# The second layer's FFN outputs: twelve of 22 k tiles by seven half-size products per pair of outputs

## The chip, the cores and the metric

The kernel runs on one core of a Trainium2 chip. The metric is the device time of one execution in microseconds (us); less is better. The engines named in the profile are TensorE (PE for its matrix products, PEld for its weight loads), VectorE (DVE), ScalarE (ACT), GpSimd (POOL) and SyncE (SP), whose queue issues most of the transfers.

## The reference, cut to what matters

A sequence of 512 tokens with 1024 features passes two layers. Each has a mixer (a gated recurrence in the first, chunked attention in the second) and a SwiGLU FFN with 2816 hidden features, each behind a norm with shift, scale and gate from a conditioning vector. A final norm gives the output. The part that matters here is the FFN of the second layer and what follows it:

```python
def swiglu(u, w_in, w_out):
    gate, up = jnp.split(u @ w_in, 2, axis=-1)
    return (jax.nn.silu(gate) * up) @ w_out
...
h = h + g2[:, None, :] * swiglu(u, ffn_w_in[layer], ffn_w_out[layer])
...
return rms_norm(h, final_norm)
```

## The kernel before

Activations lie transposed: 128 features by 512 tokens to a tile. The residual stream is eight such tiles, `h[0]` to `h[7]`; the hidden layer has 22 (`FT`), which are the k tiles of the output product. An fp32 product is made of three matmuls (`mm3`, lines 188 to 193): the weight and the activation are each split into a rounded high part and a low rest, and high·high, high·low and low·high are added into one PSUM bank. The high part is a copy on ScalarE, the low part a subtraction on VectorE (`split`, lines 124 to 137; for activations `parts`, lines 467 to 478).

Weights follow one list, `weight_plan`. `load` issues their transfers on SP's queue two ahead into a ring of three `raw` buffers; `fetch` splits them one ahead into rings of three `wh` and three `wl` buffers; `weight` hands out the next one split, and `take` hands one out raw. For one hidden tile per layer (`by_transfer`, line 120) the low part is made otherwise: ScalarE writes the negated raw weight to `wl`, and a transfer on POOL's queue adds the raw weight to it in memory (lines 131 and 132).

The FFN inputs of hidden tiles 4 to 21 (`fast_tiles`, lines 516 to 606) already use a scheme of seven products: the contraction and the tokens are cut in two, sums of weight blocks and of activation blocks are formed, and seven products with 256 tokens replace eight. Products 1 to 7 add into three banks in an order in which a bank is read by ScalarE or VectorE after each product and then added onto. Their weight buffers start at an offset of 16 elements (`NEAR`), and every fourth tile uses 24 (`APART`) for one product (line 547).

The FFN outputs (lines 480 to 513) are plain: outputs 0 and 1 run together over the 22 k tiles while those are split, then outputs 2 to 7 one after another, each from three weight chunks of 8, 8 and 6 k tiles. `residual` (line 356) adds the gated bank onto `h[n]`. `finish` (line 1382) squares the new `h[n]` into the sum for the final norm and scales the late tokens by the norm's gain (`gained`). The last output is done in two halves of the tokens: while the second half (256 products of tokens `CUT` to 511) runs, the norm of the first half is taken at its k tile 3 (`mean`) and multiplied and written at k tile 11 (`write`). `last_tokens` then transposes and writes the late tokens.

The order of instructions on each engine is made by a scheduler at build time, from priorities and dependencies; `tc.issue_after(x)` puts instructions behind x on their engine. `mods_after` in `state` is a marker of that kind.

## Time and profile before

| what | value |
|---|---|
| median of 3 runs | 1227.47 us (1226.13 to 1227.63) |
| the profiled execution | 1225.95 us, its span 1224.0 us |
| TensorE busy | 1209.0 us, 99% of the span |
| VectorE busy | 984.8 us, 80% |
| ScalarE busy | 648.4 us, 53% |
| POOL busy | 20.6 us, 2% |
| mean transfer rate | 145 GB/s, 177.55 MB |
| last fast input product, by the timeline | 1092.5 us |
| first product of the closing norm | 1214.86 us |

Matmuls overlap each other in the records, so the time of one product is read from the distance of two starts, not from its duration. A group of instructions is shown with its line, engine and operation, its operands with shapes, its count, its busy time in us and the mean of one in ns, and then the idle time ahead of it and what ended that. In the timeline a row is a start, a length, the instruction, and in brackets the idle time before it.

### The profile page before, as it was taken

How to read it: one execution, taken by the hardware profiler on the slowest of the kernel's cores; microseconds unless marked ns; L12 is line 12 of the kernel's file. 1: busy time of each engine (PE TensorE's matmuls, PEld its weight loads, DVE VectorE, ACT ScalarE, POOL GpSimd, SP SyncE). 2: the span in 40 equal slices, each digit the busy share in tenths (PEclk: the TensorE clock that was granted, in tenths of full speed). 3: DMA queues.
4: the chain of work that ended last, by engine and by line, in shares of the span. 5: the costliest groups of instructions: out<-in, count | busy, mean ns of one | idle time of the engine just before them, and what ended most of it. 6: DMA issues, size and time to landing. Idle time of an engine off the chain costs nothing.

```text
span 1224.0 us, 21555 instructions
## 1 busy us (share of the span) xinstructions
PE 1209.0 (99%) x8548; PEld 1049.3 (86%) x8548; DVE 984.8 (80%) x1769; ACT 648.4 (53%) x1157; POOL 20.6 (2%) x29
## 2 busy tenths in 40 slices
PE   8999999999999999999999999999999999999997
PEld 7887788788899999988888877777889999998887
DVE  8996778977989999987669878996798999984333
ACT  6455446443656666742228566665465666673221
POOL 0000000000000000000000000000000000000000
PEclk9999999999999999999999999999999999999999
DMA  9642354463424444568751445431243433343321
GB/s 352 255 132 97 112 183 156 155 208 121 119 91 154 155 139 141 173 208 277 235 170 69 138 139 167 164 100 58 93 120 106 153 139 138 106 128 97 100 88 69
DMA packets 52532, 177.55 MB, mean 145 GB/s; under 512 B 5968, under 2 KB 8400, under 8 KB 52432
## 3 DMA queue, kind: packets, MB, share of 16 engines
q1 hardware_dynamic: 51856, 174.08, 41.9%
q0 software_dynamic: 576, 2.10, 1.0%
q8 instruction: 67, 1.10, 0.4%
q14 instruction: 33, 0.27, 0.1%
HBM read 171.96 MB, written 2.10 MB: 142 GB/s over the span
## 4 chain that ended last, share of the span: by engine, by line
PE 90%; DVE 5%; ACT 3%; issue 1%; DMA 1%; SPq 0%; POOL 0%; DVEq 0%; POOLq 0%; ACTq 0%
PE f_r L561 9%; PE f_r L560 9%; PE f_r L559 9%; PE f_o L193 6%; PE f_o L192 6%; PE f_o L191 6%; PE f L191 2%; PE f L193 2%; PE f L192 2%; PE o L859 1%; PE bo L1271 1%; PE bo L191 1%; PE av L214 1%; PE bo L193 1%; PE bo L192 1%; PE ao L191 1%
## 5 line engine op out<-in xcount | busy, mean ns | idle before, releaser
L561 PE MATMUL f_r<-f_h,f_w_l 128*128 128x256 f32 x1008 | 279.0, 277 | 0.0
L559 PE MATMUL f_r<-f_h,f_w_h 128*128 128x256 f32 x1008 | 278.7, 277 | 0.0
L560 PE MATMUL f_r<-f_l,f_w_h 128*128 128x256 f32 x1008 | 278.7, 277 | 0.0
L561 PEld LDWEIGHTS f_r<-f_h,f_w_l 128*128 128x128 f32 x1008 | 189.3, 188 | 0.4 <-DVE f_w_l L525 0.4
L560 PEld LDWEIGHTS f_r<-f_l,f_w_h 128*128 128x128 f32 x1008 | 189.5, 188 | 0.1
L559 PEld LDWEIGHTS f_r<-f_h,f_w_h 128*128 128x128 f32 x1008 | 189.3, 188 | 0.1
L192 PE MATMUL f_o<-f_p,f_o_h 128*128 128x512 f32 (+1 forms) x374 | 141.1, 377 | 0.1
L193 PE MATMUL f_o<-f_p,f_o_l 128*128 128x512 f32 (+1 forms) x374 | 141.2, 378 | 0.0
L191 PE MATMUL f_o<-f_p,f_o_h 128*128 128x512 f32 (+1 forms) x374 | 140.8, 377 | 0.0
L127 ACT ACTIVATE f_o_h<-r_f_o 128x1024 fp32r<-128x1024 f32 (+1 forms) x48 | 46.8, 987 | 131.5 <-PE f_o L192 98.2
L341 DVE SCALAR_TENSOR_TENSOR mw<-mw,crow 128x1024 f32<-128x1024 f32 x96 | 115.3, 1217 | 0.7 <-DMA mw<-in_modw 0.7
L134 DVE TENSOR_TENSOR f_o_l<-r_f_o,f_o_h 128x1024 fp32r<-128x1024 f32 (+1 forms) x48 | 54.1, 1132 | 67.9 <-ACT f_o_h L127 60.4
L524 ACT ACTIVATE f_w_h<-f_x 128x1024 fp32r<-128x1024 f32 x72 | 76.7, 1065 | 46.1 <-PE f_r L560 39.0
L525 DVE TENSOR_TENSOR f_w_l<-f_x,f_w_h 128x1024 fp32r<-128x1024 f32 x72 | 87.8, 1224 | 4.8 <-ACT f_w_h L524 2.4
L524 ACT ACTIVATE f_w_h<-r_f_c 128x1024 fp32r<-128x1024 f32 x72 | 61.1, 849 | 46.0 <-PE f_r L560 44.9
L193 PEld LDWEIGHTS f_o<-f_p,f_o_l 128*128 128x128 f32 x374 | 70.3, 188 | 14.3 <-DVE f_o_l L134 1.5
L192 PEld LDWEIGHTS f_o<-f_p,f_o_h 128*128 128x128 f32 x374 | 70.4, 188 | 13.3 <-DVE f_p L476 0.6
L191 PEld LDWEIGHTS f_o<-f_p,f_o_h 128*128 128x128 f32 x374 | 70.4, 188 | 12.8
L525 DVE TENSOR_TENSOR f_w_l<-r_f_c,f_w_h 128x1024 fp32r<-128x1024 f32 x72 | 68.5, 951 | 5.8 <-ACT f_w_h L524 5.8
L1246 ACT ACTIVATE sb<-sb,st 128x128 f32<-128x128 f32 (+1 forms) x64 | 35.8, 560 | 29.8 <-DVE st L1245 29.4
L762 DVE TENSOR_TENSOR kq<-kq,t 128x1024 f32<-128x1024 f32 x28 | 34.2, 1220 | 5.2 <-PE fine L786 2.6
L193 PE MATMUL f<-f_h,f_l 128*128 128x512 f32 x96 | 36.9, 391 | 0.0
(401 smaller groups left out, 2705.5 us busy)
## 6 DMA issues: line engine op xcount, KB each, us to landing
mw<-in_modw SPq DMA_DIRECT2D x96, 512.0 KB, 4.2
r_f_c<-in_ffn_in SPq DMA_DIRECT2D x72, 512.0 KB, 3.4
r_f_o<-in_ffn_out SPq DMA_DIRECT2D x32, 512.0 KB, 3.6
mrow<-in_modw SPq DMA_DIRECT2D x16, 512.0 KB, 8.5
r_f<-in_ffn_in SPq DMA_DIRECT2D x16, 512.0 KB, 3.4
r_f_o<-in_ffn_out SPq DMA_DIRECT2D x16, 384.0 KB, 3.4
r_av<-in_a_v SPq DMA_DIRECT2D x8, 512.0 KB, 4.6
r_g<-in_a_g SPq DMA_DIRECT2D x8, 512.0 KB, 3.3
```

What stands on the lines that cost most here:

```text
L127: A.activation(wh, raw, AF.Copy)
L134: low = V.tensor_sub(wl, raw, wh)
L191: T.matmul(ps, wh[:, kt, :], uh, start=start, stop=False)
L192: T.matmul(ps, wh[:, kt, :], ul, start=False, stop=False)
L193: T.matmul(ps, wl[:, kt, :], uh, start=False, stop=stop)
L341: V.scalar_tensor_tensor(mw, mw, 1.0, crow, op0=ALU.mult, op1=ALU.mult, accum_out=raw[:, j:j + 1])
L524: A.activation(wh, raw, AF.Copy)
L525: V.tensor_sub(wl, raw, wh)
L559: T.matmul(ps, wh[:, j, :], uh, start=f, stop=False, skip_group_check=True)
L560: T.matmul(ps, wh[:, j, :], ul, start=False, stop=False, skip_group_check=True)
L561: T.matmul(ps, wl[:, j, :], uh, start=False, stop=stop and j == 3, skip_group_check=True)
L1246: A.activation(s[:, 0:n], s[:, 0:n], AF.Exp, bias=st[:, 1:2], accum_out=st[:, 2:3])
```

## The change

Only the second layer's FFN outputs change (`OUT` = 1).

- K tiles 0 to 11 (`PAIRS` = 6 pairs) are done by seven half-size products for each pair of outputs (2i, 2i+1): the two outputs, the two k tiles of a pair and the two halves of the tokens are the blocks. Products 1, 5, 6, 2, 7, 3, 4 add into three banks r1, r2, r3; after each one VectorE adds the bank onto the one quarter of `h` that it belongs to, with the sign from `g2` or `ng2`.
- K tiles 12 to 21 stay plain, in two chunks of five. Outputs 0 and 1 run them together, then outputs 2 to 5 (their low weight parts now by adding transfers); then come the four pairs; then the plain part of outputs 6 and 7 (`HELD`) in halves of the tokens, early tokens of 7 and 6, then late tokens of 6 and 7.
- While outputs 2 to 5 run, `prepare_pairs` forms two sums (y0, y2) of activation quarters for each of the six pairs of k tiles, two quarters in each, and splits all seven operands.
- `weights` prepares seven weight operands per pair of outputs, three products ahead. Of their four sums, two are made by transfers (`load_sum`: SP loads one block from HBM into a tile, then a POOL transfer adds another block from HBM to it), two by VectorE. The next pair's sum is asked for once this pair's is used.
- The norm's `mean` comes at step 5 of the 20 steps of the last two half outputs (it was 3 of 22), `write` at step 11 as before. `gained` uses one tile for two outputs.
- The weights of k tiles 0 to 11 lie in HBM with the even k tiles first.

The diff, cut to its core:

```diff
-CUT, WRITE_AT = 256, 11
+CUT, MEAN_AT, WRITE_AT = 256, 5, 11
...
+OUT, PAIRS, CHUNK = 1, 6, 5
+HELD, FREE = (6, 7), 14
...
     def by_transfer(key):
+        if key[0] == f"f{OUT}" and key[1] == "o":
+            return 2 <= key[2] < HELD[0]
         return key[0] in [f"f{layer}" for layer in FAST] and key[1] == PLAIN - 1
     def split(raw, nk, n, nm, tag, key):
-        wh = wp.tile([P, nk, n], F32R, tag=tag + "h", name=f"{nm}_h")
-        wl = wp.tile([P, nk, n], F32R, tag=tag + "l", name=f"{nm}_l")
+        if key in spare:
+            wh, wl = spare.pop(key)()
+        elif key[:2] == (f"f{OUT}", "o") and key[2] in HELD:
+            wh, wl = (wp.tile([P, SHIFT + D], F32R, tag=tag + x, name=f"{nm}_{x}")[:, NEAR:NEAR + nk * n]
+                      .rearrange("p (k c) -> p k c", k=nk) for x in "hl")
+        else:
+            wh = wp.tile([P, nk, n], F32R, tag=tag + "h", name=f"{nm}_h")
+            wl = wp.tile([P, nk, n], F32R, tag=tag + "l", name=f"{nm}_l")
         A.activation(wh, raw, AF.Copy)
         state.pop("meanwhile", lambda: None)()
         if by_transfer(key):
             A.activation(wl, raw, AF.Copy, scale=-1.0)
-            G.dma_start(out=wl, in_=raw, accum_op=ALU.add)
+            state["moved"] = G.dma_start(out=wl, in_=raw, accum_op=ALU.add)
         else:
             low = V.tensor_sub(wl, raw, wh)
...
+            if layer == OUT:
+                drain(side)
+                fast_out(fp, nm, a, raw_a, FIRST, g2, finish)
+                return
...
+    def fast_out(fp, nm, a, raw_a, first, g2, finish):
+        H = S // 2
+        row1, row2 = slice(H, S), slice(0, H)
+        K0 = 2 * PAIRS
+        halves = (slice(0, CUT), slice(CUT, S))
+        room = [(cst, f"ul{i}", 1) for i in range(8)] + [(cst, "uh4", 1), (cst, "uh5", 1)]
+        room = [(fp, f"sp{i}", 1) for i in range(10)] + room + [(fp, "sp10", 1), (cst, "uh6", 1), (cst, "uh7", 1)]
+        room += [(mp, "mraw", 2), (mp, "mraw", 2), (mp, "crow", 2), (fp, "xs1", 4), (fp, "xs0", 4), (fp, "ab0", 2)]
+        units = []
+        def unit():
+            if not units:
+                pool, tag, m = room.pop(0)
+                kw = {"bufs": 2} if tag == "mraw" else {"bufs": 1}
+                t = pool.tile([P, m, S], F32R, tag=tag, name=f"{nm}_u{len(room)}", **kw)
+                units.extend(t[:, i, :] for i in range(m))
+            return units.pop(0)
+        def split_plain(k):
+            if not isinstance(a[k], tuple):
+                ah, al = unit(), unit()
+                A.activation(ah, a[k], AF.Copy)
+                with tc.issue_after(ends[min(FREE + k - K0, len(ends) - 1)].ins):
+                    V.tensor_sub(al, a[k], ah)
+                a[k] = ah, al
+            return a[k]
+        order = (2, 5, 3, 4, 0, 1)
+        sums_at = dict(zip(order, ("uo0", "uo1", "uo2", "uo3", "xs2", "xs3")))
+        slots = {}
+        def pair(j):
+            k = 2 * j
+            base = k if k < first else first + 4 * ((k - first) // 4)
+            return raw_a[base][:, k - base:k - base + 2, :]
+        def two(x):
+            return x.rearrange("p (a c) -> p a c", a=2)
+        def prepare_pairs():
+            for j in order:
+                r = pair(j)
+                y0 = sm.tile([P, 2, H], F32, tag="et", name=f"{nm}_y{j}", bufs=2)
+                y2 = sm.tile([P, 2, H], F32, tag="ut", name=f"{nm}_z{j}", bufs=2)
+                with tc.issue_after(state["mods_after"].ins):
+                    V.tensor_sub(y0[:, 0, :], r[:, 1, row2], r[:, 0, row2])
+                    V.scalar_tensor_tensor(y0[:, 1, :], y0[:, 0, :], -1.0, r[:, 0, row1], op0=ALU.mult, op1=ALU.subtract)
+                yield
+                with tc.issue_after(state["mods_after"].ins):
+                    V.tensor_sub(y2[:, 0, :], r[:, 0, row1], r[:, 0, row2])
+                    V.scalar_tensor_tensor(y2[:, 1, :], r[:, 1, row1], -1.0, y0[:, 1, :], op0=ALU.mult, op1=ALU.subtract)
+                yield
+                t = fp.tile([P, 8, H], F32R, tag=sums_at[j], name=f"{nm}_q{j}")
+                for i, y in enumerate((y0, y2)):
+                    A.activation(t[:, 2 * i:2 * i + 2, :], y, AF.Copy)
+                    V.tensor_sub(t[:, 4 + 2 * i:6 + 2 * i, :], y, t[:, 2 * i:2 * i + 2, :])
+                    yield
+                oh, ol, m = two(unit()), two(unit()), two(unit())
+                A.activation(oh, r[:, :, row1], AF.Copy)
+                A.activation(m[:, 0, :], r[:, 1, row2], AF.Copy)
+                with tc.issue_after(state["mods_after"].ins):
+                    V.tensor_sub(ol, r[:, :, row1], oh)
+                    V.tensor_sub(m[:, 1, :], r[:, 1, row2], m[:, 0, :])
+                slots[j] = {1: (oh[:, 0, :], ol[:, 0, :]), 3: (oh[:, 1, :], ol[:, 1, :]), 2: (m[:, 0, :], m[:, 1, :])}
+                slots[j].update({4 + i: (t[:, i, :], t[:, 4 + i, :]) for i in range(4)})
+                yield
+        ops = {}
+        def one(i, q, raw):
+            at = APART if q == 7 and i % 2 == 0 else NEAR
+            wh, wl = (wp.tile([P, SHIFT + D], F32R, tag="w" + x, name=f"{nm}_o{i}_{q}{x}")[:, at:at + PAIRS * P]
+                      .rearrange("p (j c) -> p j c", j=PAIRS) for x in "hl")
+            A.activation(wh, raw, AF.Copy)
+            V.tensor_sub(wl, raw, wh)
+            ops[i, q] = wh, wl
+        added = {}
+        def load_sum(i, q):
+            if i < 4:
+                t = fp.tile([P, PAIRS, P], F32, tag={1: "x2", 3: "ab2"}[q], name=f"{nm}_t{q}_{i}")
+                odd, even = slice(PAIRS, 2 * PAIRS), slice(0, PAIRS)
+                w = d["ffn_out"][OUT]
+                with tc.issue_after(state["asked"].ins):
+                    nc.sync.dma_start(t, w[2 * i + 1, :, even, :])
+                with tc.issue_after(state["moved"].ins):
+                    G.dma_start(out=t, in_=w[2 * i, :, even, :] if q == 1 else w[2 * i + 1, :, odd, :], accum_op=ALU.add)
+                added[i, q] = t
+        def weights(i):
+            def got(x):
+                return take((nm, "o", i, x))
+            one(i, 1, got("c11"))
+            yield
+            t1 = added.pop((i, 1))
+            one(i, 5, t1)
+            yield
+            b22 = got("c22")
+            t2 = fp.tile([P, PAIRS, P], F32, tag="x1", name=f"{nm}_t2_{i}")
+            V.tensor_add(t2, b22, t1)
+            one(i, 6, t2)
+            load_sum(i + 1, 1)
+            yield
+            b21 = got("c21")
+            one(i, 2, b21)
+            V.tensor_add(t2, b21, t2)
+            yield
+            one(i, 7, added.pop((i, 3)))
+            load_sum(i + 1, 3)
+            yield
+            one(i, 3, b22)
+            yield
+            one(i, 4, t2)
+            yield
+        def stream():
+            for i in range(4):
+                yield from weights(i)
+        chunks = stream()
+        done = {"n": 0}
+        def ahead(upto):
+            while done["n"] < upto and next(chunks, chunks) is not chunks:
+                done["n"] += 1
+        def product(i, q, ps, s, start):
+            wh, wl = ops.pop((i, q))
+            for j in range(PAIRS):
+                uh, ul = slots[j][s]
+                f = start and j == 0
+                T.matmul(ps, wh[:, j, :], uh, start=f, stop=False, skip_group_check=True)
+                T.matmul(ps, wh[:, j, :], ul, start=False, stop=False, skip_group_check=True)
+                T.matmul(ps, wl[:, j, :], uh, start=False, stop=j == PAIRS - 1, skip_group_check=True)
+        def onto(n, c, ps):
+            g = ng2 if n % 2 else g2
+            V.scalar_tensor_tensor(h[n][:, c], ps, g[:, n:n + 1], h[n][:, c], op0=ALU.mult, op1=ALU.add)
+        ng2 = cst.tile([P, KT], F32, tag="ng2", name="ng2")
+        with tc.issue_after(ends[-1].ins):
+            V.tensor_scalar_mul(ng2, g2, -1.0)
+        prep = prepare_pairs()
+        load_sum(0, 1)
+        pss = [bank(f"{nm}_o{n}_0") for n in range(2)]
+        for ci in range(2):
+            ws = [weight((nm, "o", n, ci)) for n in range(2)]
+            for kt in range(CHUNK):
+                k = K0 + CHUNK * ci + kt
+                for k2 in (k, min(k + 1, FT - 1)):
+                    split_plain(k2)
+                for w, ps in zip(ws, pss):
+                    mm3(ps, w, kt, a[k], k == K0, k == FT - 1)
+        for n, ps in enumerate(pss):
+            residual(n, ps, g2)
+        for n in range(2, HELD[0]):
+            ps = bank(f"{nm}_o{n}_0")
+            for ci in range(2):
+                w = weight((nm, "o", n, ci))
+                for kt in range(CHUNK):
+                    k = K0 + CHUNK * ci + kt
+                    mm3(ps, w, kt, a[k], k == K0, k == FT - 1)
+                    if kt != 2:
+                        next(prep, None)
+                    if n == HELD[0] - 1 and ci and kt in (1, 3):
+                        ahead((kt + 1) // 2)
+            residual(n, ps, g2)
+            if n == HELD[0] - 1:
+                load_sum(0, 3)
+        drain(prep)
+        def beside():
+            t = fp.tile([P, 2, D], F32R, tag="uo0", name=f"{nm}_o6_w")
+            return [t[:, e, NEAR:NEAR + CHUNK * P].rearrange("p (k c) -> p k c", k=CHUNK) for e in range(2)]
+        spare[nm, "o", HELD[0], 1] = beside
+        for i in range(4):
+            n0, n1 = 2 * i, 2 * i + 1
+            r1, r2, r3 = (bank(f"{nm}_or{q}_{i}")[:, 0:H] for q in (1, 2, 3))
+            for at, (q, ps, s, start, n, c) in enumerate((
+                    (1, r1, 1, True, n0, row1), (5, r2, 4, True, n1, row2), (6, r1, 5, False, n1, row1),
+                    (2, r3, 3, True, n0, row1), (7, r1, 6, False, n1, row2), (3, r2, 7, False, n1, row1),
+                    (4, r1, 2, False, n0, row2))):
+                ahead(7 * i + at + 3)
+                product(i, q, ps, s, start)
+                onto(n, c, ps)
+            if n0 not in HELD:
+                finish(n0, slice(0, S))
+                finish(n1, slice(0, S))
+        ws = {n: [weight((nm, "o", n, ci)) for ci in range(2)] for n in HELD[::-1]}
+        later, step = {}, 0
+        for c, ns in zip(halves, (HELD[::-1], HELD)):
+            for n in ns:
+                ps = bank(f"{nm}_o{n}_{c.start}h")
+                for ci in range(2):
+                    for kt in range(CHUNK):
+                        k = K0 + CHUNK * ci + kt
+                        if c.start and step in later:
+                            later.pop(step)()
+                        step += bool(c.start)
+                        mm3(ps[:, c], ws[n][ci], kt, [x[:, c] for x in a[k]], k == K0, k == FT - 1)
+                residual(n, ps, g2, c)
+                later = finish(n, c) or later
...
     def finish(n, c):
-        if c.start:
+        if c.start and n == KT - 1:
             last_tokens()
             return None
         square_into(acc, n, "n4", c)
-        if n < KT - 1:
+        if n < KT - 1 and c.stop == S:
             gained(n)
+        if n != HELD[0] or c.stop == S:
             return None
         got = {}
...
-        return {3: mean, WRITE_AT: write}
+        return {MEAN_AT: mean, WRITE_AT: write}
...
+    def out_plan(nm, layer):
+        def plain(n, ci):
+            k0 = 2 * PAIRS + CHUNK * ci
+            one((nm, "o", n, ci), d["ffn_out"][layer, n, :, k0:k0 + CHUNK, :], CHUNK)
+        for ci in range(2):
+            for n in range(2):
+                plain(n, ci)
+        for n in range(2, HELD[0]):
+            for ci in range(2):
+                plain(n, ci)
+        for i in range(4):
+            for x, c, e in (("c11", 0, 0), ("c22", 1, 1), ("c21", 0, 1)):
+                one((nm, "o", i, x), d["ffn_out"][layer, 2 * i + c, :, e * PAIRS:(e + 1) * PAIRS, :], PAIRS)
+        for n in HELD[::-1]:
+            for ci in range(2):
+                plain(n, ci)
```

More of the change, by code (lines that the diff above doesn't have):

```diff
@@ L141, in trunk @@
     ready = {}
-    shifts, partial = {}, {}
+    shifts, partial, spare = {}, {}, {}
     state = {"loaded": 0, "split": 0, "used": 0}
@@ L151, in load @@
             raws[key] = wp.tile([P, nk, n_], F32, tag="raw", name=f"r_{nm}")
-            nc.sync.dma_start(raws[key], src)
+            state["asked"] = nc.sync.dma_start(raws[key], src)
             state["loaded"] += 1
@@ L158, in fetch @@
             ahead += 1
-        while state["split"] < min(i + ahead + 1, len(plan)) and plan[state["split"]][0][-1] not in ("c1", "c2"):
+        while state["split"] < min(i + ahead + 1, len(plan)) and str(plan[state["split"]][0][-1])[0] != "c":
             key, _, nk, n = plan[state["split"]]
@@ L564, in fast_tiles @@
         done = {"n": 0}
+        ends.clear()
         def ahead(upto):
@@ L600, in fast_tiles @@
             last = V.tensor_mul(row2, row2, p5)
+            ends.append(last)
             kept(n, at)
@@ L606, in fast_tiles @@
         fetch(state["used"] - 1, 1)
+    ends = []
+    def fast_out(fp, nm, a, raw_a, first, g2, finish):
[183 more added lines that the diff above has]
+                later = finish(n, c) or later
@@ L1373, in trunk @@
     tail = out[D * CUT:D * S].rearrange("(b p d) -> b p d", p=P, d=D)
-    hw = []
+    hw, held = [], {}
     def gained(n):
-        t = cst.tile([P, S], F32, tag=f"uh{n}", name=f"hw{n}", bufs=1)[:, 0:S - CUT]
+        if n % 2 == 0:
+            held["t"] = cst.tile([P, 2, S - CUT], F32, tag=f"uh{n // 2}", name=f"hw{n}", bufs=1)
+        t = held["t"][:, n % 2, :]
         A.activation(t, h[n][:, CUT:S], AF.Copy, scale=cols[:, C_FIN + n:C_FIN + n + 1])
@@ L1452, in ffn @@
         order = [(n, c) for c in chunks for n in range(first)] + [(n, c) for n in range(first, KT) for c in chunks]
+        if layer == OUT:
+            out_plan(nm, layer)
+            return
         for n, (ci, (k0, nk)) in order:
@@ L1527, in _layout @@
     r["ffn_in"] = np.ascontiguousarray(fi)
-    r["ffn_out"] = np.stack([_blocks(w) for w in a["ffn_w_out"]])
+    fo = np.stack([_blocks(w) for w in a["ffn_w_out"]])
+    fo[OUT] = fo[OUT][:, :, list(range(0, 2 * PAIRS, 2)) + list(range(1, 2 * PAIRS, 2)) + list(range(2 * PAIRS, FT)), :]
+    r["ffn_out"] = fo
     r["b_k"] = _blocks(a["kv_w"][:, :D])
```

## The prediction

> **What bounds the kernel now.** I read the page first: busy time, slices, the chain that ended last.
>
> ```profile
> span 1224.0 us, 21555 instructions
> PE 1209.0 (99%) x8548; PEld 1049.3 (86%) x8548; DVE 984.8 (80%) x1769; ACT 648.4 (53%) x1157; POOL 20.6 (2%) x29
> ...
> DVE  8996778977989999987669878996798999984333
> ...
> PEclk9999999999999999999999999999999999999999
> ...
> PE 90%; DVE 5%; ACT 3%; issue 1%; DMA 1%; SPq 0%; POOL 0%; DVEq 0%; POOLq 0%; ACTq 0%
> ```
>
> TensorE is 90% of the chain, at full clock. VectorE, near nine tenths in most slices, falls to three or four tenths in the last four: these are the second layer's FFN outputs, where the change works. A change there pays if it shortens TensorE's row of products, and as long as what it hands to VectorE, ScalarE and the queues stays under that row.
>
> A busy PE overstates each product, because products overlap. What counts is the step from one start to the next. The view by windows gives it (columns: stretch, length, then busy us and instructions of PE, weight loads, VectorE, ScalarE, POOL; clock, DMA share, GB/s).
>
> ```profile
> 1123.00:1197.00 74.00, 74.00 (x328) 61.29 (x327) 24.81 (x27) 21.21 (x28) 0.00 (x0) 1.00 0.30 91
> ...
> 930.00:1092.00 162.00, 161.98 (x1426) 161.78 (x1425) 152.28 (x237) 100.13 (x173) 0.00 (x0) 1.00 0.38 130
> ```
>
> Each window counts about two products that only overlap its edges. So a 512-column product of the outputs takes 74/326 = 0.227 us, and a 256-column product of the fast input tiles 162/1424 = 0.1138 us, half of it, although VectorE was 94% busy beside them. A half-size product costs half: that is the ground of the forecast.
>
> That pace is not the only one. These are starts in the timeline of PE: the first two with 12 products between them, just after the step from 512 to 256 columns; the next two with 30, in output 7, already cut in halves.
>
> ```profile
> 920.26 0.28 PE L559 MATMUL f_r<-f_h,f_w_h 128*128 128x256 f32 x1
> ...
> 921.68 0.28 PE L559 MATMUL f_r<-f_h,f_w_h 128*128 128x256 f32 x1
> ...
> 1211.15 0.28 PE L193 MATMUL f_o<-f_p,f_o_l 128*128 128x256 f32 x1
> ...
> 1214.74 0.28 PE L193 MATMUL f_o<-f_p,f_o_l 128*128 128x256 f32 x1
> ```
>
> 1.42/12 = 0.118 and 3.59/30 = 0.120 us: a slower pace, 4 to 5% above the other.
>
> The stage to be changed runs from the last fast input product to the first product of the closing norm:
>
> ```profile
> 1092.40 0.28 PE L560 MATMUL f_r<-f_l,f_w_h 128*128 128x256 f32 x1
> ...
> 1214.86 0.50 PE L1416 MATMUL n_ss_last<-mean,acc 128*128 128x1 f32 x4
> ```
>
> One product follows the first row, so the outputs take about 1214.86 − 1092.52 = 122.3 us. They have 7 × 22 × 3 = 462 products at 0.227 (104.9) and 132 at 0.120 (15.8): 120.7. The other 1.6 us are waits at the start and the small products of the norm.
>
> **The change, part by part.** *TensorE.* Every output keeps ten plain k tiles: outputs 0 to 5 have 6 × 10 × 3 = 180 products at 0.227 = 40.9 us; outputs 6 and 7, in halves at the end, 120 at 0.114 to 0.120, I take 13.9. The other twelve k tiles of eight outputs were 8 × 12 × 3 = 288 full products (65.4 us); they become 4 pairs × 7 products × 6 k × 3 = 504 half ones at 0.1138 = 57.4 us. Changing from 512 to 256 columns begins in the slow pace, until the first product with the other weight offset: 72 × 0.0045 = 0.3. Sum 112.5, with the old 1.6 us of small things 114.1. Gross gain 122.3 − 114.1 = 8.2 us. All this is on the path.
>
> *VectorE and ScalarE.* Durations by form, from the groups of lines after 1070 us:
>
> ```profile
> L476 DVE TENSOR_TENSOR f_p<-f_ar,f_p 128x512 fp32r<-128x512 f32 x18 | 11.2, 681 | 0.0
> L134 DVE TENSOR_TENSOR f_o_l<-r_f_o,f_o_h 128x768 fp32r<-128x768 f32 x8 | 7.6, 950 | 6.2 <-PE f_o L193 6.2
> L357 DVE SCALAR_TENSOR_TENSOR h<-f_o,mod_g2b,h 128x512 f32<-128x512 f32 x7 | 5.2, 751 | 15.3 <-PE f_o L193 15.3
> ...
> L238 DVE TENSOR_TENSOR acc<-acc,n_sq 128x512 f32<-128x512 f32 x6 | 4.1, 683 | 0.0
> ...
> L357 DVE SCALAR_TENSOR_TENSOR h<-f_o,mod_g2b,h 128x256 f32<-128x256 f32 x2 | 1.0, 484 | 6.4 <-PE f_o L193 6.4
> ...
> L595 DVE TENSOR_TENSOR f_ar<-f_qu 128x256 f32<-128x256 f32 x2 | 0.8, 418 | 0.0
> ```
>
> ```profile
> L475 ACT ACTIVATE f_p<-f_ar 128x512 fp32r<-128x512 f32 x18 | 10.0, 621 | 1.4 <-DVE f_p L476 1.2 <-DVE f_w_l L525 0.2
> L127 ACT ACTIVATE f_o_h<-r_f_o 128x768 fp32r<-128x768 f32 x8 | 6.7, 843 | 20.9 <-PE f_o L192 20.9
> ...
> L1379 ACT ACTIVATE hw<-h,cols 128x256 f32<-128x256 f32 x8 | 4.0, 496 | 7.2 <-DVE h L357 7.2
> L235 ACT ACTIVATE n_sq<-h 128x512 f32<-128x512 f32 x6 | 3.8, 630 | 0.8 <-DVE h L357 0.8
> ```
>
> In a pair, VectorE has seven low parts and two weight sums of 768 columns (9 × 0.950), seven additions onto the residual (7 × 0.484) and two norm sums (2 × 0.683): 13.3 us beside 126 × 0.1138 = 14.3 of TensorE, 93%. The fast tiles carried 94% without holding TensorE, so I cost it at nothing. If that cover went, each pair would lose the overhang. ScalarE has 7 × 0.843 + 2 × (0.630 + 0.496) = 8.2 us. Every addition onto h must have read its bank before the bank's next product; one whole product (18 × 0.1138 = 2.05 us) lies between, over four times the 0.484.
>
> Under outputs 0 to 5 (40.9 us) VectorE prepares the six pairs of k tiles, each five halves at 0.418 and three of 512 columns at 0.681: 4.1, in all 24.8. It also has ten plain splits (6.8), four low parts of 640 columns (3.3, between the rows of 512 and 768) and six residuals (4.5): 39.4 us. At 94% that is 41.9, so 0 to 1.0 us may show; back to back they overlap a little, and two splits already fall under the last tiles. I take 0.3.
>
> *The transfers of outputs 2 to 5.* Their eight low weight parts leave VectorE: ScalarE writes −w_h and a POOL transfer adds the raw weight. The trace has this for one fast input weight of 1024 columns (tile f_l, from 895 us; the last line is the time from issue to landing):
>
> ```profile
> L131 ACT ACTIVATE f_l<-r_f x2: 1047/1050/1052, 903.7 to 907.2; 128x1024 fp32r<-128x1024 f32 x2
> L132 POOL DMA_DIRECT2D f_l<-r_f x2: 859/890/922, 905.1 to 908.6; - x2
> ...
>   DMA f_l<-r_f: 0.2, 1
> ...
> DMA to landing us min/median/max: 4.6/5.0/5.5
> ```
>
> A buffer comes free at the start of a chunk and must be full again two chunks later, 2 × 15 × 0.227 = 6.8 us. The refill: two casts of 640 columns (0.73 each, between 0.621 and 0.843), 0.3 to the issue (907.2 + 1.05 to 908.55), landing 4.6 to 5.5: 6.4 to 7.3 us, with whatever ScalarE has queued ahead. With three buffers TensorE loses a third of the excess per chunk: 8 × 0.5/3 = 1.3 at 7.3 us, and with two casts in front (1.5 us more) 5.3. Ends 0 and 5.3; a transfer of 320 KB should be nearer the short end of a 512 KB one, so I take 1.0. The raw weight's buffer too is held until the transfer lands, so the next load on SP waits for it.
>
> The SBUF — State Buffer page of the Trainium skill, section "SBUF: two separate sides", warns that VectorE in a two-port mode keeps POOL from writing the descriptors of such a DMA. The 0.86 to 0.92 us of POOL's two issues, made while VectorE was at work, show no such stretch. By that page's example, about 3.1 us where 0.62 were enough, each refill would be late by an estimated 2.5 us and the sum 8 × 2.5/3 = 6.7 us worse; by the row it is nothing.
>
> *The two sums by transfer.* Each is a load by SP and an adding transfer by POOL straight from HBM, into one buffer per sum. No adding transfer from HBM is in the trace: it lands between 3.0 us (the plain load below) and twice the longest seen, 11; nearest is the 5.0 of f_l, which I take.
>
> ```profile
> r_f_o<-in_ffn_out SPq DMA_DIRECT2D x6, 384.0 KB, 3.0
> ```
>
> The third product's buffer is the tighter: cast and low part 1.8 us; then its load stands on SP behind a weight load that waits one more product, 2.05; load 3.0; transfer 5.0: 11.9 us in a period of 14.3. It is hidden, up to a landing of 7.4 us. Past that, each of three changes of pair loses the excess.
>
> *The end.* The norm's mean now comes 5 steps after the first halves, the write 6 steps later instead of 8; a step is 3 × 0.12 = 0.36 us, and output 6's second half needs VectorE in between.
>
> ```profile
> 1207.52 0.61 PE L243 MATMUL n_ss<-mean,acc 128*128 128x1 f32 x4
> ...
> 1209.32 0.48 DVE L261 TENSOR_SCALAR n_dg<-ident,n_rs 128x128 f32<-128x128 f32 x2 [1.85 <-POOL n_rs L252]
> 1210.47 0.60 PE L262 MATMUL n_rb<-n_dg,ones 128*128 128x128 f32 x4
> 1211.11 3.22 DVE L1401 SCALAR_TENSOR_TENSOR yo<-h,cols,n_rb 128x256 f32<-128x256 f32 x8 [1.31 <-PE n_rb L262]
> ```
>
> From n_ss to the end of n_dg are 2.3 us, and 6 × 0.36 + 0.36 = 2.5 remain: no wait, unless the residual of output 6 (0.48) goes first. Then the eight yo (3.22 + 0.64) just fill the nine steps that are left. Between 0 and 0.9 us lost; I take 0.4. What follows stays.
>
> Edits at nothing: the reordered weights in memory (the host's layout), the k order, ng2, and two-per-tile outputs for the norm, which change no instruction's length.
>
> *Sum*: 8.2 − 0.3 − 1.0 − 0.4 = 6.5 us; 0.2 more for some forty products at the slow pace after those waits leaves 6.3. The profiled execution took 1225.95 us (1.95 around its span), 1.5 below the median 1227.47; the four times shown have a mean of 1226.8. 1225.95 − 6.3 = 1219.65; against the mean, 1220.5, which I forecast.
>
> **The rivals.** (a) *Part of the gain is eaten by feeding*: refills with ScalarE's casts ahead cost 5.3 instead of 1.0 and VectorE 1.0 instead of 0.3, so 1220.5 + 5.0 = 1225.5. The same comes if POOL's issue of a refill has to stand behind two VectorE operations of 0.950: 8 × 1.9/3 = 5.1. For it: ScalarE has 16 × 0.73 = 11.7 us of these casts besides the preparation, in one queue. Against: 0.2 us of wait in the f_l row, and POOL's 0.86 to 0.92.
>
> (b) *Slower: adding transfers from HBM land late.* At 11 us the third product's cycle is 17.9 against 14.3, 3 × 3.6 = 10.8 lost: 1231.3. The gain is gone from a landing of 7.4 + 6.3/3 = 9.5 us. Against: 5.5 is the longest here. The casts that wait stand in ScalarE's one queue, and VectorE's low parts behind them.
>
> (c) *Weight loads become the bound.* If a 128-row load could not run under the product before it, every half product would last its load:
>
> ```profile
> L559 PEld LDWEIGHTS f_r<-f_h,f_w_h 128*128 128x128 f32 x1008 | 189.3, 188 | 0.1
> ```
>
> 504 × 0.188 = 94.8 instead of 57.4: 1258. The row of 1426 products in 162 us speaks against it. The page TensorE: Matmul & The Clock Gate of the Trainium skill, section "The mechanism", says loads overlap products in flight only where they use other row groups, which would be this case; the step of 0.1138 us disagrees.
>
> (d) *Nothing is left to feed late, and TensorE has no new wait*: 1226.8 − 8.2 = 1218.6.
>
> **How the numbers follow.** The forecast 0.58 (1219 to 1223), (d) 0.10, (a) 0.18, (b) 0.12, (c) 0.02. The timings shown scatter by 0.1%, so 0.2% (2.5 us) is about what can be told from no change: 1224.3 to 1229.3 is "same". Of (a) a third is faster (up to 1224.3), two thirds the same: faster 0.58 + 0.10 + 0.06 = 0.74, same 0.12, slower 0.14. The range goes from (d) less the 0.9 us by which the lowest time shown lies under the mean, 1217.7, to 1 us past (a), 1226.5; I give 1217.5 to 1226.5. It leaves out (b), (c) and a few ends.
>
> **What would show it.** Right: half products at 0.114 us in the pairs, with only the first four products near 0.118; the outputs about 116 us long; VectorE near 0.9 in the pairs and PE without waits. Wrong: PE waiting for an added weight part in outputs 2 to 5 (refill above 6.8 us); ScalarE waiting for a sum's transfer (landing above 7.4); PE waiting for pair sums of activations when the pairs begin; VectorE late for a residual bank.

## The result, and the profile after

The changed kernel takes 1239.35 us (median of four, 1237.57 to 1239.49) where the kernel before takes 1227.37 (four, 1226.13 to 1227.63): a ratio of 1.0096, interval 1.0079 to 1.0114. It is slower by 12 us; 1220.5 was forecast. The profiled execution took 1239.49 us. Its page, with span, busy time, slices and chain:

```profile
span 1237.7 us, 22215 instructions
PE 1219.9 (99%) x8758; PEld 1066.1 (86%) x8758; DVE 1028.2 (83%) x1856; ACT 670.2 (54%) x1198; POOL 35.3 (3%) x45
...
DVE  8986768977989999987668778996788999988775
...
PEclk9999999999999999999999999999999999999999
...
PE 90%; DVE 4%; DMA 2%; issue 2%; ACT 2%; POOL 0%; DVEq 0%; POOLq 0%; ACTq 0%
```

The page hides the cause. VectorE now works through the last slices, as intended; the clock shows nine tenths or more in every slice; TensorE is still 99% busy and 90% of the chain. A TensorE that is busy all the time can still be slower at the same work, and that shows in starts. In the timeline of PE of the changed kernel, the first and the last product of the fast input tiles of layers 0 and 1, the first product of the pairs, and the first of the closing norm:

```profile
343.85 0.28 PE L575 MATMUL f_r<-f_h,f_w_h 128*128 128x256 f32 x1
...
521.82 0.28 PE L577 MATMUL f_r<-f_h,f_w_l 128*128 128x256 f32 x1
...
930.26 0.28 PE L575 MATMUL f_r<-f_h,f_w_h 128*128 128x256 f32 x1
...
1108.36 0.28 PE L577 MATMUL f_r<-f_h,f_w_l 128*128 128x256 f32 x1
...
1151.36 0.29 PE L763 MATMUL f_or<-f_u,f_o_1h 128*128 128x256 f32 x1
...
1228.16 0.50 PE L1646 MATMUL n_ss_last<-mean,acc 128*128 128x1 f32 x4
```

The same view of the kernel before: layer 0's first and last fast product, and four starts in layer 1's first tile.

```profile
340.62 0.28 PE L559 MATMUL f_r<-f_h,f_w_h 128*128 128x256 f32 x1
...
512.91 0.28 PE L561 MATMUL f_r<-f_h,f_w_l 128*128 128x256 f32 x1
...
927.33 0.28 PE L559 MATMUL f_r<-f_h,f_w_h 128*128 128x256 f32 x1
...
928.74 0.28 PE L559 MATMUL f_r<-f_h,f_w_h 128*128 128x256 f32 x1
...
929.09 0.28 PE L559 MATMUL f_r<-f_h,f_w_h 128*128 128x256 f32 x1
...
931.47 0.28 PE L559 MATMUL f_r<-f_h,f_w_h 128*128 128x256 f32 x1
```

The changed stage got shorter: from the end of the fast tiles to the norm 1228.16 − 1108.47 = 119.7 us, where it was 1214.86 − 1092.62 = 122.2. What got longer is work that the change doesn't touch. Layer 0's fast tiles go from 172.3 to 178.0 us and layer 1's from 172.2 to 178.1. With 3.2 us more before layer 0's tiles, 1.1 between the layers, 0.4 behind the norm's first product and 2.6 less in the outputs that is 3.2 + 5.7 + 1.1 + 5.9 − 2.6 + 0.4 = 13.7, the difference of the spans.

How the two kernels differ in the fast tiles is in the windows of PE, which hold nothing but 256-column products (stretch, length, busy us and count, clock, DMA share, GB/s). Before:

```profile
360.00:510.00 150.00, 149.98 (x1320) 1.00 0.42 143
950.00:1050.00 100.00, 99.98 (x879) 1.00 0.40 138
```

After:

```profile
360.00:510.00 150.00, 150.00 (x1276) 1.00 0.43 138
950.00:1050.00 100.00, 100.00 (x851) 1.00 0.43 141
```

Less the two products that only overlap the edges, a product took 150/1318 = 0.1138 us and now takes 150/1274 = 0.1177, at the same clock 1.00 and without a wait. The rows of the kernel before, above, show that it has both paces: from 920.26 to 928.74, 72 products, the step is 0.1178; from 929.09 to 931.47, 21 products, it is 0.1133. It changes where the last of the tile's seven half-size products begins, at 928.74. The one whose weights lie at the other offset (`APART`) is the sixth: its 12 matmuls, from 927.33 to 928.74, still ran at 1.41/12 = 0.1175. So the fast pace sets in right behind it, as the weights go back to the first offset. After the change the place is passed too, and the step stays at 0.118.

### The profile page after: what moved, and what is told of

Read it like the earlier page. It is cut to its first block, busy times and chain, and to the rows that moved or that the text cites. A ratio compares the mean times of both kernels' runs of the same rounds, so it can differ in the third digit from the quotient of the medians.

```text
span 1237.7 us, 22215 instructions
## 1 busy us (share of the span) xinstructions
PE 1219.9 (99%) x8758; PEld 1066.1 (86%) x8758; DVE 1028.2 (83%) x1856; ACT 670.2 (54%) x1198; POOL 35.3 (3%) x45
## 4 chain that ended last, share of the span: by engine, by line
PE 90%; DVE 4%; DMA 2%; issue 2%; ACT 2%; POOL 0%; DVEq 0%; POOLq 0%; ACTq 0%
PE f_r L577 10%; PE f_r L575 10%; PE f_r L576 9%; PE f_o L205 3%; PE f_o L204 3%; PE f_o L203 3%; PE f L204 2%; PE f L203 2%; PE f L205 2%; PE o L1086 1%; PE bo L1498 1%; PE av L226 1%; PE f_or L763 1%; PE f_or L764 1%; PE bv L226 1%
## 5 line engine op out<-in xcount | busy, mean ns | idle before, releaser
L575 PE MATMUL f_r<-f_h,f_w_h 128*128 128x256 f32 x1008 | 284.7, 282 | 0.0
L577 PE MATMUL f_r<-f_h,f_w_l 128*128 128x256 f32 x1008 | 283.3, 281 | 0.0
L577 PEld LDWEIGHTS f_r<-f_h,f_w_l 128*128 128x128 f32 x1008 | 193.2, 192 | 0.0
L139 ACT ACTIVATE f_o_h<-r_f_o 128x1024 fp32r<-128x1024 f32 (+2 forms) x39 | 34.4, 890 | 72.7 <-PE f_o L204 53.5
L204 PE MATMUL f_o<-f_p,f_o_h 128*128 128x512 f32 x176 | 68.6, 390 | 0.1
L205 PE MATMUL f_o<-f_p,f_o_l 128*128 128x512 f32 x176 | 68.7, 390 | 0.0
L203 PE MATMUL f_o<-f_p,f_o_h 128*128 128x512 f32 x176 | 68.4, 389 | 0.0
L146 DVE TENSOR_TENSOR f_o_l<-r_f_o,f_o_h 128x1024 fp32r<-128x1024 f32 (+2 forms) x31 | 32.8, 1062 | 21.2 <-ACT f_o_h L139 20.1
L204 PEld LDWEIGHTS f_o<-f_p,f_o_h 128*128 128x128 f32 x176 | 33.0, 188 | 7.4 <-DVE f_p L492 0.6
L205 PEld LDWEIGHTS f_o<-f_p,f_o_l 128*128 128x128 f32 x176 | 33.0, 188 | 7.4 <-DVE f_o_l L146 0.5
L203 PEld LDWEIGHTS f_o<-f_p,f_o_h 128*128 128x128 f32 x176 | 33.0, 188 | 6.7
L204 PE MATMUL f<-f_l,f_h 128*128 128x512 f32 x96 | 37.4, 397 | 0.0
```

The costliest lines, as they stand in the source:

```text
L139: A.activation(wh, raw, AF.Copy)
L203: T.matmul(ps, wh[:, kt, :], uh, start=start, stop=False)
L204: T.matmul(ps, wh[:, kt, :], ul, start=False, stop=False)
L205: T.matmul(ps, wl[:, kt, :], uh, start=False, stop=stop)
L575: T.matmul(ps, wh[:, j, :], uh, start=f, stop=False, skip_group_check=True)
L577: T.matmul(ps, wl[:, j, :], uh, start=False, stop=stop and j == 3, skip_group_check=True)
```

## The experiments

My theory: the new tile `ng2` lies at the end of the first pool of buffers, so its 32 bytes per partition move every buffer of the later pools, among them the fast tiles' weights and high-part activations, while the low parts of the activations, in the first pool, stay. TensorE's pace for these products depends on the addresses. The rival: the new code itself, by its transfers and its order, slows TensorE. All ratios are to runs of the kernel before on the same chip.

**1. ng2 where an old tile was.** The addresses are then those of before, and the rest of the change stays.

```diff
-        ng2 = cst.tile([P, KT], F32, tag="ng2", name="ng2")
+        ng2 = sm.tile([P, KT], F32, tag="lbt", name="ng2")
```

> The changed kernel with its one new 32-byte tile (ng2) put into a buffer that was there already, so that every buffer behind it has the address that it had before the change. Theory A (addresses): the tile moved all later buffers by 32 bytes, and the slow pace of TensorE (0.1178 us per half product instead of 0.1133, in both layers' fast tiles, and some us in the stages ahead) comes from that: the fast tiles return to 0.1133, the outputs begin at 1092.5 us as before, and the time falls by 15.9 us to 1223.5 (ratio to before about 0.997). Theory B (the new work itself slows TensorE: other instruction order, more transfers): the tile does not matter, the time stays at 1239.

1223.08 us (1222.43 to 1223.63), ratio 0.9965 [0.9952, 0.9977]: faster than before. Windows of PE:

```profile
360.00:510.00 150.00, 149.99 (x1299) 1.00 0.41 138
950.00:1050.00 100.00, 100.00 (x881) 1.00 0.42 143
```

100/879 = 0.1138 in layer 1; in layer 0 two stretches of tiles run at the slow pace, each from a half-size product that took longer than the others up to the next one at the other offset (1299 lies between 1276 and 1320). Not every such delay ends the fast pace: in the kernel before, the eleventh tile has one too, 0.1392 per matmul, and went on at 0.1133. One line of placement makes 16 us.

**2 and 3. The kernel before with an unused tile of 32 or of 64 bytes** at the end of the same pool, and nothing of the change.

```diff
+    V.memset(cst.tile([P, 8], F32, tag="room", name="room"), 0.0)
```

(with 16 in place of 8 for 64 bytes)

> The kernel before, with nothing added but one unused 32-byte tile at the end of the first pool (and its memset of under 0.2 us). Theory A: the slow pace appears in the old kernel too: fast tiles at 0.1178 us, time 1227.4 + 15.9 or more, about 1243 to 1248 (its long plain outputs slow down as well). Theory B: 1227.4, no change.

> The kernel before with an unused tile of 64 bytes there. If theory A holds and only the place within 64 bytes counts, the pace is the old one, 0.1133, and the time 1227.4. If any move of the buffers counts, or their distance to the tiles of the first pool which do not move, it is slow, 1239 to 1248. Theory B: 1227.4.

1241.42 us, 1.0115 [1.0100, 1.0131], and 1243.06, 1.0127 [1.0113, 1.0141]. Windows of PE with 32 bytes:

```profile
360.00:510.00 150.00, 150.00 (x1276) 1.00 0.40 140
```

and with 64:

```profile
360.00:510.00 150.00, 150.00 (x1265) 1.00 0.40 138
```

The count of the changed kernel returns to the product with 32 bytes, and 64 give 150/1263 = 0.1188. So the whole loss comes without the change, from a tile that nothing reads. The rival has fallen.

**4 and 5. Which address?** The changed kernel with its weight offsets 8 elements lower has the weights where they were before, and the high parts of the activations 32 bytes on. The kernel before with offsets 8 higher moves the weights alone.

```diff
-NEAR, APART, EVERY = 16, 24, 4
+NEAR, APART, EVERY = 8, 16, 4
```

(24, 32 in the kernel before)

> The changed kernel with the offsets of the half-size weights lowered from 16 and 24 to 8 and 16 elements, so that those weights alone stand at the old places within 64 bytes while all else stays moved by 32. If the place of the weights decides the pace, the fast tiles return to 0.1133 in both layers (11.4 us): about 1228. If it is the place of the activations or of both to each other, it stays at 0.1178 and 1239.

> The kernel before with the two offsets of the half-size weights raised from 16 and 24 to 24 and 32 elements: the weights of the fast tiles move by 32 bytes, nothing else moves. In e4 weights at the old place with moved activations were slow. If it is the distance of weights and activations that counts, the fast tiles are slow here too, 0.1178 in both layers, 1227.4 + 11.4 = 1239; if only the place of the activations counts, 1227.4.

1237.35 us, 1.0082 [1.0068, 1.0096], and 1237.66, 1.0081 [1.0068, 1.0094]. Windows of PE, first with the offsets 8 lower in the changed kernel:

```profile
360.00:510.00 150.00, 150.00 (x1276) 1.00 0.40 139
```

then with 8 higher in the kernel before:

```profile
360.00:510.00 150.00, 150.00 (x1272) 1.00 0.43 140
```

Both are slow. Weights at the old address don't bring the pace back, and weights moved alone lose it, so it is not the weights' own address alone. Nor is it one distance alone: experiment 2 leaves weights and high parts as they lay to each other, experiment 4 weights and low parts, experiment 5 high and low parts, and all three are slow. That it hangs on how the three lie to each other fits all of this. The pairs fit it too, the other way round: in the changed kernel they reached the fast pace (126 matmuls from 1161.96 to 1176.28, 0.1137), and with the offsets 8 lower, where nothing but weights moved, they did not (126 from 1165.72 to 1180.64, 0.1184).

**6 and 7. How far?** The kernel before with 128 and with 256 bytes of unused room (32 and 64 elements).

> The kernel before with an unused tile of 128 bytes at the end of the first pool. 32 bytes and 64 bytes were slow (fast tiles 0.1178 and 0.1188). If the pace depends on the distance of moved and unmoved buffers within 128 bytes, this one is fast, 0.1133 and 1227; if any other distance than the present one is slow, 1239 to 1243.

> The same with 256 bytes: fast, 1227, if the distance counts within 256 bytes or within 128; slow, 1239 to 1243, if it counts in full.

1241.87 us (two runs), 1.0121 [1.0103, 1.0138], and 1226.95 (eight), 0.9996 [0.9986, 1.0006]. Windows of PE, 128 bytes:

```profile
360.00:510.00 150.00, 150.00 (x1276) 1.00 0.43 139
```

256 bytes:

```profile
360.00:510.00 150.00, 149.98 (x1320) 1.00 0.44 143
```

256 bytes cost nothing, so the loss is not that of a fuller or a shifted memory as such: the position within 256 bytes counts.

**8. Is the pace switched, or is it a property of each offset?** The kernel before with one weight offset for all products.

```diff
-NEAR, APART, EVERY = 16, 24, 4
+NEAR, APART, EVERY = 16, 16, 4
```

> The kernel before with both offsets of the half-size weights at 16 elements, so that no product uses another one. Theory E (the pace is a state, which a product from the other offset switches): the slow pace of the first fast tile, 0.1175, stays through both layers' fast tiles, about 1227.4 + 11.5 = 1239. If the pace follows from the place of each product's own operands, all tiles after the first stay at 0.1133: 1227.

1237.32 us (two runs), 1.0084 [1.0066, 1.0101]. Windows of PE:

```profile
360.00:510.00 150.00, 150.00 (x1276) 1.00 0.43 138
```

Every weight lies at an offset that runs at 0.1138 in the kernel before, and here it runs at 0.1177 throughout. So the pace is one that TensorE keeps, and in the kernel before it is the passage through the other offset and back that moves it to the faster one.

**What the outputs wait for.** With the addresses set aside, the stage took 116.3 us in experiment 1 and 119.7 in the changed kernel. What is lost inside it stands in the changed kernel's waits (who waits, for whom, us, times, longest):

```profile
DVE f_t L731 <- DMA f_t<-in_ffn_out: 3.0, 1, 3.0
...
PEld f_or L763 <- ACT f_o_5h L703: 2.4, 1, 2.4
...
PE f_or L763 <- DVE h L769: 2.2, 1, 2.2
```

and its timeline tells how they hang together (rows from the queues of SP, POOL, VectorE, ScalarE and TensorE):

```profile
1166.01 0.33 SPq L715 DMA_DIRECT2D f_t<-in_ffn_out  x1
...
1171.81 0.86 POOL L717 DMA_DIRECT2D f_t<-in_ffn_out  x1 [8.66 <-DMA f_t<-in_ffn_out]
...
1179.17 0.96 DVE L731 TENSOR_TENSOR f_t<-r_f_o_c,f_t 128x768 f32<-128x768 f32 x1 [3.00 <-DMA f_t<-in_ffn_out]
...
1180.05 0.48 DVE L769 SCALAR_TENSOR_TENSOR h<-f_or,ng,h 128x256 f32<-128x256 f32 x1
...
1180.67 0.36 PE L763 MATMUL f_or<-f_u,f_o_4h 128*128 128x256 f32 x1 [2.18 <-DVE h L769]
```

The first sum of the third pair was asked for at 1166.01; its load took 5.8 us and its adding transfer 7.3. VectorE, waiting for it at the head of its queue, held back the addition of a bank onto `h` that was ready, and TensorE waited 2.2 us for that bank. The wait cost more than itself. The clock in a window of PE around it is no longer full (stretch, length, busy us and count, clock, DMA share, GB/s):

```profile
1140.00:1200.00 60.00, 57.69 (x437) 0.97 0.76 186
```

Within it the granted clock is 0.50 from 1182 to 1184, and from 1181.75 to 1184.95 a matmul took 3.20/15 = 0.213 us instead of 0.114: about 1.5 us more. Experiment 1, with a wait of 1.5 us in the same place, kept 1.00 from 1140 to 1195. Four experiments, all on top of experiment 1, try to take this away.

**9. The first sum asked for earlier.** A second buffer for it, and the request moved from the third weight of the pair to the first.

```diff
-    t = fp.tile([P, PAIRS, P], F32, tag={1: "x2", 3: "ab2"}[q], name=f"{nm}_t{q}_{i}")
+    t = fp.tile([P, PAIRS, P], F32, tag={1: ("x2", "ab1")[i % 2], 3: "ab2"}[q], name=f"{nm}_t{q}_{i}")
...
             one(i, 1, got("c11"))
+            load_sum(i + 1, 1)
...
             one(i, 6, t2)
-            load_sum(i + 1, 1)
```

> On top of e1 (addresses as before): the first product's weight sum t1 gets a second buffer (ab1, free by then) and is asked for one pair earlier in the list, with the first product instead of the third. Theory C (the waits of TensorE in the pairs come from this sum landing late: 1.7 us for f_o_5h and 1.5 us for the bank that VectorE, held by the same sum, read late): both waits go, the 504 half products shrink from 59.8 to about 57 us, time 1223.1 - 2.7 = 1220.4. Theory D (those waits come from VectorE's load, 93% of the stage): they stay, 1223.

1225.57 us, scattered from 1220.57 to 1229.04 over twelve, ratio 0.9979 [0.9966, 0.9993]: no better than experiment 1, and the outputs took 120.9 us. Its waits:

```profile
ACT f_o_7h L703 <- DMA f_t<-in_ffn_out: 7.9, 1, 7.9
...
PE f_or L763 <- ACT f_o_4h L703: 4.8, 1, 4.8
```

The later pairs have no wait any more, but in the first pair POOL's one queue has the next pair's first sum ahead of this pair's second one, and the loads of both went out together at 1133.13. The two adding transfers were issued at 1137.53 and 1139.82; ScalarE waits 7.9 us for the later one, TensorE 4.8, and after that the granted clock is 0.50 from 1150 to 1152. The scatter goes with the clock in part: the three runs with a mean clock of 0.998 or more took 1220.57 to 1223.36 us, the four with 0.996 took 1226.40 to 1228.90.

**10. Both sums by VectorE**, from blocks already loaded. The sums take w[2i, odd] where w[2i+1, even] belongs, so that one load of 384 KB per pair is not made.

```diff
-            t1 = added.pop((i, 1))
+            V.tensor_add(t1, b21, b11)
...
-            one(i, 7, added.pop((i, 3)))
+            V.tensor_add(t3, b21, b22)
+            one(i, 7, t3)
```

> On top of e1: the two weight sums of each pair of outputs are made by VectorE from the three raw weights that are loaded anyway, not by a load and an adding transfer each (16 transfers fewer). Theory C: no wait for a sum, but VectorE gets 2 x 0.95 more per pair, 15.2 us nominal in 14.3 of TensorE; if operations follow each other at 0.87 it still fits and the time is 1220 to 1221, else TensorE loses up to 0.9 x 4 = 3.6 in place of 3.2, about 1223.5. Theory D: clearly slower than e1, 1226 or more.

1224.18 us, 0.9970 [0.9959, 0.9981], outputs 118.9 us. No sum waits for an adding transfer, but in the first pair VectorE stood 4.5 us for a plain block of weights that its first sum needs, and that pair took 16.9 us. Two more sums of 768 columns per pair bring VectorE to 13.3 + 2 × 0.950 = 15.2 us beside TensorE's 14.3: the second pair still took 14.5, and the third and fourth, with a wait of 0.5 us each and slow steps behind it, 15.3 and 15.4:

```profile
DVE f_t L729 <- DMA r_f_o_c<-in_ffn_out: 5.5, 4, 4.5
...
PE f_or L764 <- DVE h L770: 1.0, 2, 0.5
...
PE f_or L766 <- DVE f_o_5l L704: 0.9, 1, 0.9
```

**11. The low parts of outputs 2 to 5 by VectorE**, none by transfers.

```diff
-            return 2 <= key[2] < HELD[0]
+            return False
```

> On top of e1: the low weight parts of outputs 2 to 5 by VectorE, as for the other outputs, not by ScalarE and adding transfers. The recorded sum had 39.4 us of VectorE under the 40.9 us of outputs 0 to 5; with eight low parts of 0.82 it is 46.0. If that count is right TensorE waits about 4 us more when the pairs begin, less the 1 us that it waits for a transfer in e1: about 1226. If VectorE follows on at its back-to-back pace (0.89 of the durations) it fits, and the time is that of e1 or 1 us less, 1222.

1226.88 us, 0.9998 [0.9990, 1.0007], outputs 122.4 us. The plain outputs run without a wait in 40.9 us, but what VectorE was to have done by the start of the pairs comes late there:

```profile
DVE f_t L731 <- DMA f_t<-in_ffn_out: 4.7, 1, 4.7
...
PE f_or L763 <- DVE h L769: 3.9, 1, 3.9
...
PE f_or L765 <- DVE f_o_1l L704: 2.0, 1, 2.0
```

The outputs took 6.1 us more than in experiment 1, but not all of that is VectorE's load. The 2.0 us are; the 3.9 us stand behind a late sum once more, the second pair's, and after them the granted clock is 0.50 from 1156 to 1160. The four runs with a mean clock of 0.995, the profiled one among them, took 1227.82 to 1230.92 us, the other six 1225.56 to 1227.14. By the two ratios, 0.9998 against 0.9965, the adding transfers earn their place with some 4 us.

**12. Both sums earlier.** Experiment 9, and the first pair's second sum asked for at the start of output 5 instead of its end, so that it stands ahead of the others in POOL's queue.

```diff
+            if n == HELD[0] - 1:
+                load_sum(0, 3)
...
-            if n == HELD[0] - 1:
-                load_sum(0, 3)
```

> e5 with the first pair's second sum (t3) asked for at the start of output 5, so that it does not stand on POOL's queue behind the second pair's first sum, which waits for the buffer ab1: in e5 that cost 5.0 and 1.4 us in the first pair's fourth and fifth product. Theory C: no wait for a sum is left, the 504 half products take 57 to 58 us (59.8 in e1), time 1220 to 1221. Theory D (VectorE's load): about 3 us of waits remain, 1223.

1220.98 us (1219.18 to 1222.44), ratio 0.9948 [0.9936, 0.9960]: faster than both kernels. Against experiment 1 the intervals overlap a little; the outputs in the traces separate them. Timeline of PE, last fast product, first and last of the pairs, first of the norm:

```profile
1095.95 0.28 PE L577 MATMUL f_r<-f_h,f_w_l 128*128 128x256 f32 x1
...
1137.90 0.28 PE L763 MATMUL f_or<-f_u,f_o_1h 128*128 128x256 f32 x1
...
1195.44 0.28 PE L765 MATMUL f_or<-f_u,f_o_4l 128*128 128x256 f32 x1
...
1210.24 0.50 PE L1646 MATMUL n_ss_last<-mean,acc 128*128 128x1 f32 x4
```

The only wait of its TensorE in the stage:

```profile
PE f_o L205 <- DMA f_o_l<-r_f_o: 0.7, 1, 0.7
```

The outputs take 114.2 us, 8.1 less than before, and the pairs 57.6. Some of that is given back ahead: the fast tiles of layer 1 took 174.7 us here, 2.5 more than before, with a wait of 0.8 us for VectorE in the third tile and the slow pace behind it.

## Why the prediction was wrong, and where it was right

**The step that failed** is the line "Edits at nothing: the reordered weights in memory (the host's layout), the k order, ng2, and two-per-tile outputs for the norm, which change no instruction's length". `ng2` changes the step of a third of the program's products: 0.0039 us on each of 2 × 18 × 84 fast input products is 11.8 us (11.6 measured), and the other stretches ahead of the outputs lost 4.3 more (3.2 + 1.1). In experiment 2, with the unused bytes alone, these stretches lost nearly the same, 2.8 + 1.1. All my rivals lay inside the outputs. I had seen both paces and quoted them, had even named the product at the other offset as what ends the slow one, and gave it 0.3 + 0.2 us. What I did not ask is whether that switch still works after the change: the buffers' addresses were part of the change.

**The late sums** were the second miss, in size and in place. I sized the load at 3.0 us and the transfer at 5.0, called the third product's sum the tighter, and found both hidden. In the third pair the first sum's load took 5.8 and its transfer 7.3. In the mechanism (landings in time or not) I was right, and the transfers stayed within its bounds of 3.0 to 11; but a median of single loads doesn't hold beside the pairs' other transfers. The summary of the landings of this tile in the changed kernel, loads and adding transfers mixed:

```profile
DMA to landing us min/median/max: 3.0/4.9/7.3
```

I had also written that VectorE would be hidden at 93%; it is, in experiment 12 (46.0 us busy in 55 of the pairs). What I had not asked is what stands behind a waiting VectorE in its one queue, and what a wait does to the clock: the sum takes TensorE at full clock throughout.

**Right, once the addresses were as before:**

- *A half product at half cost.* Experiment 12's pairs take 57.6 us for 504 products, where I had 57.4 + 0.3. The first five of the first pair's seven run at the slow pace, where I had four: the fifth is the one at the other offset, and as in the fast tiles the pace changes behind it.
- *The size of the gain.* "Outputs about 116 us": 116.3 in experiment 1; the gross 114.1: 114.2 in experiment 12. By time, experiment 1 gives 0.9965 and experiment 12 0.9948, where my 1220.5 against 1226.8 was 0.9949. That they fit so closely is in part luck. In experiment 1 the pairs took 59.8 us where I had 57.7, and the rest of the stage 56.5 where I had 58.3. Experiment 12 is not the kernel that I forecast, and its time holds 3.3 us that its fast tiles lost (0.8 in layer 0, 2.5 in layer 1). My 122.3 for the outputs before counts from the start of the last fast product; from its end they take 122.2.
- *Refills by adding transfers* in outputs 2 to 5 at 1.0 us (0 to 5.3): TensorE waits 0.7, in one place. They land 3.7 to 6.0 us after their issue; POOL's issue is 0.86 us while VectorE works, as it was for the one weight that was made so before. Rival (a) did not come.
- *Weight loads* (rival (c)) bind nothing: steps of 0.1133 beside loads of 0.188 in the pairs too (18 in 2.04 us).

## What to carry to other kernels

A new tile, however small, is an edit to the addresses of every buffer that is allocated after it. When a stage that wasn't touched changes its pace at a full clock and without waits, compare the step between starts in it, then put the new tile where an old one was, or pad the kernel before by the same bytes: two runs separate placement from the change. Where several adding transfers share one queue, ask for them in the order in which they are used, and look at what stands behind the engine that waits for them. After a wait of TensorE, read the granted clock in narrow windows: the row of slices hid the half clock here.

## What the runs showed of the hardware that I had not expected

TensorE ran the same 128 by 256 fp32 product at two paces, 0.1133 to 0.1138 and 0.1177 to 0.1188 us, at the same clock. The faster one was reached, in the kernel before, just behind the half-size product whose weights lie 32 bytes further, and then kept; that product itself took 0.1175 per matmul in the slow pace, and 0.1200 to 0.1208 in the fifth, ninth, thirteenth and seventeenth tile, where the others had 0.1133. Moving the later pools, the weights and the high parts together, by 32, 64 or 128 bytes against the low parts kept TensorE from reaching it; 256 bytes did not. It is worth 10 to 16 us of 1227 in this kernel.

The page TensorE: Matmul & The Clock Gate of the Trainium skill, section "Step-by-step: what each phase is for", says that TensorE reads weights and streamed operands through two independent ports, so that loading the next weights takes nothing from the running product. The sentence does not speak of addresses; if the ports were all, the place of the weights should not matter. Here moving the weights alone by 32 bytes (the kernel before with offsets 8 higher) made each product 4% longer, and the measurement decides.

TensorE's waits of 2.2, 3.9 and 4.8 us (the changed kernel, experiments 11 and 9) were each followed by a granted clock of 0.50 for some us, those of 1.5 and 2.0 us (experiments 1 and 11) were not.

What makes the two paces, why the passage through the other offset switches them, and which of the three distances counts, no run here shows. Distances other than these were not tried, nor a product at the other offset more often than every fourth tile.
